# Reciprocal roots of the norms: ten VectorE steps replaced by one GpSimd power, and some diagonals made on ScalarE

## The chip, the core and the metric

The kernel runs on one core of one Trainium2 chip. The engines are named as the profile names them: PE (TensorE matmul; PEld is its weight load), DVE (VectorE), ACT (ScalarE), POOL (GpSimd) and SP (SyncE, which here issues nearly all DMAs). Each engine works through its own queue in order, and the queues wait for each other through semaphores. The metric is the device time of one execution in microseconds.

## What is computed

Two transformer layers on 512 rows of 1024 channels, with 256 rows of context beside them in the first layer. Layer 0 mixes with a gated chunk MLP and a differential attention of four heads; layer 1 with a windowed attention of 16 heads. Each layer ends in a SwiGLU of 2816 hidden channels. What matters here is the norm in front of nearly everything:

```python
def rmsnorm(x, g):
    xf = x.astype(jnp.float32)
    y = xf * lax.rsqrt(jnp.mean(xf * xf, axis=-1, keepdims=True) + EPS)
    return (y * g.astype(jnp.float32)).astype(x.dtype)
```

It stands at the entry of each layer, before each FFN, on the output of each head of layer 0 (over 128 channels), and at the end. The chunk MLP has a variance norm of its own, `lax.rsqrt(mean((vf - mu)^2) + EPS)`.

## The kernel before, in words

The activations lie transposed: a tile holds 128 channels on the partitions and up to 512 (rows) or 256 (context) positions along the free axis. Products are made in three passes (`mm3`, L99 to L101): a value is split into a high part in a reduced format, cast on ACT (L75, L115, L901), and a low rest, subtracted on POOL or DVE (L78, L116, L904), and high x high, high x low and low x high are summed. So every weight tile passes ACT and then POOL (or DVE) before PE can use it.

**A norm** has five steps. ACT squares the tiles and DVE or POOL add them up (`squares`, `square`, L183 and L769, L185 and L773). `rstd_diag` (L138) multiplies each block of 128 positions of the sums by a matrix of ones on PE (L149, L153), which leaves the sum of squares of position p on partition p; one DVE instruction takes the needed column of each block, scales it and adds epsilon (L156, or L158 for the heads, whose epsilon is a tensor). Then `rsqrt_small` (L124) takes the reciprocal root of these few columns, one per block of 128 positions: 2, 3, 4 or 6 of them. It starts from the bit trick (L128) and makes three Newton rounds of three DVE instructions each (L130, L131, L132), every one reading the one before. A diagonal matrix is built from each column by multiplying the identity with it, on DVE (L165). `spread` (L171) multiplies ones by the diagonals on PE (L175), which puts the factors of all positions on all partitions; the modulation or scaling reads them from there (L191, L599, L831, L1257, L1259).

There are 14 such norms, in order of time: rows and context at the entry (4 and 2 columns); the four heads of layer 0 (6 each); two halves before the FFN of layer 0 (3 each); rows and context at the entry of layer 1 (4 and 2); two halves before the FFN of layer 1 (2 each); two halves at the end (2 each). The chunk MLP calls the same `rsqrt_small` once through `rstd_small` (L118) on 24 columns.

**The FFN** (L842 on) computes each hidden tile f with a fast scheme of seven products (numbered 1 to 7) on sums and differences of the weights' and the inputs' quarters. The sums of weights are DVE instructions (L925). The second half's norm comes first in its order, "r", followed by products 2 and 1 of the tiles 0 to 2, which need only the first half; product 5 is the first that needs the second half modulated. In layer 0 the sums for product 5 of the first three tiles are tied behind the last diagonal of the norm:

```python
with tc.issue_after(self.last_diag.ins) if both and f < 3 and n == 5 else ExitStack():
    nc.vector.tensor_tensor(t, x, y, how)
```

**What sets the order.** The program is written for a tile framework, opened with `schedule_with_timeline_sim=True`. At build it simulates the engines with its own costs, gives an engine the ready instruction that stands earliest in the program (blocks under `high_priority` count as earlier), and so fixes the order of every queue; `issue_after` adds an edge by hand. On the chip that order doesn't change any more. An instruction that waits holds all that its engine has behind it.

Of the kernel before, what the change touches and what calls it, by code (L numbers as in the profile page):

```python
# [6 lines left out]
F32 = mybir.dt.float32  # L7
F32R = mybir.dt.float32r
BF16 = mybir.dt.bfloat16
I32 = mybir.dt.int32  # L10
AF = mybir.ActivationFunctionType
ALU = mybir.AluOpType
AX = mybir.AxisListType.X

P = 128
# [7 lines left out]
EPS = 1e-6  # L23
# [3 lines left out]
class Builder:  # L27
# [94 lines left out]
        return self.rsqrt_small(v, n, tag, 3)  # L122

    def rsqrt_small(self, v, n, tag="sm", bufs=6):  # L124

        ve = self.nc.vector
        y, t = self.small(n, tag, bufs), self.small(n, tag, bufs)
        ve.tensor_scalar(y.bitcast(I32), v.bitcast(I32), -0.5, float(0x5F3759DF), ALU.mult, ALU.add)  # L128
        for _ in range(3):
            ve.tensor_tensor(t, y, y, ALU.mult)  # L130
            ve.scalar_tensor_tensor(t, t, -0.5, v, ALU.mult, ALU.mult)  # L131
            ve.scalar_tensor_tensor(y, t, 1.5, y, ALU.add, ALU.mult)  # L132
        return y

    def rstd_rows(self, acc, T, inv, bank=None, dg=None, more=(), out=None):
# [2 lines left out]
    def rstd_diag(self, accs, inv, bank=None, eps=None, at=None, more=()):  # L138

        nc = self.nc  # L140
        nb = sum(T for _, T in accs) // P
        ms = self.small(nb)
        o = 0
        for acc, T in accs:
            ps = (bank or self.bank)()
            n = T // P
            for j in range(n):
                c = slice(j * P, (j + 1) * P)
                nc.tensor.matmul(ps[:, c], acc[:, c], self.ones, start=j == 0, stop=not more, skip_group_check=True)  # L149
            for t in more:  # L150
                for j in range(n):
                    c = slice(j * P, (j + 1) * P)
                    nc.tensor.matmul(ps[:, c], t[:, c], self.ones, start=False, stop=t is more[-1], skip_group_check=True)  # L153
            col = ps[:, 0:T].rearrange("p (j f) -> p j f", f=P)[:, :, 0]
            if eps is None:
                nc.vector.tensor_scalar(ms[:, o:o + n], col, inv, EPS, ALU.mult, ALU.add)  # L156
            else:
                nc.vector.scalar_tensor_tensor(ms[:, o:o + n], col, inv, eps[:, o:o + n], ALU.mult, ALU.add)  # L158
            o += n
        r = self.rsqrt_small(ms, nb)  # L160
        dgs, o = [], 0
        for acc, T in accs:
            dg = at if at is not None else self.tmp()
            for j in range(T // P):
                self.last_diag = nc.vector.tensor_scalar(dg[:, j * P:(j + 1) * P], self.ident, r[:, o + j:o + j + 1], None,  # L165
                                                         ALU.mult)
            dgs.append(dg[:, :T])
            o += T // P
        return dgs
# [119 lines left out]
    def consts(self):  # L289
        nc, a, p0 = self.nc, self.a, self.p0  # L290
        self.acc = [p0.tile([P, 96], F32, name=f"acc{i}") for i in range(2)]
        self.mod = [p0.tile([P, 96], F32, name=f"mod{i}") for i in range(2)]
        self.ones = p0.tile([P, P], F32, name="ones")
        nc.gpsimd.memset(self.ones, 1.0)
        warm = p0.tile([P, 1], F32, name="warm")
        nc.scalar.activation(warm, self.ones[:, 0:1], AF.Silu)

# [544 lines left out]
    def ffn(self, l):  # L842
        tc, nc, a = self.tc, self.nc, self.a
        both = l == 0
# [53 lines left out]
        def slot(src, t=None):  # L898
            t = ring.tile([P, 2, 512], F32R, name=self.uid("w"), tag="w", bufs=(6, 10)[l]) if t is None else t
            with tc.issue_after(self.first_sq.ins) if self.nslot < 12 else ExitStack():  # L900
                nc.scalar.copy(t[:, 0, :], src)  # L901
            self.nslot += 1
            eng = nc.vector if l == 1 and self.nslot % 4 == 0 else nc.gpsimd
            eng.tensor_tensor(t[:, 1, :], src, t[:, 0, :].bitcast(F32), ALU.subtract)  # L904
            return t
# [9 lines left out]
        def weights(n, f):  # L915
            if f not in raws:
                raws[f] = self.raws.pop(f) if f < 2 else self.ffn_in(l, f, ring if f % 3 == 2 else self.Rf)
                sums[f] = self.sumsq()[:, :512] if f % 3 == 2 else self.tmp("t")
            r, t = raws[f], sums[f]
            a11, a12, a21, a22 = [r[:, i * 512:(i + 1) * 512] for i in range(4)]  # L920
            for v, x, y, how in ((5, a21, a22, ALU.add), (6, t, a11, ALU.subtract), (3, a12, t, ALU.subtract),
                                 (7, a11, a21, ALU.subtract)):
                if v == n:
                    with tc.issue_after(self.last_diag.ins) if both and f < 3 and n == 5 else ExitStack():
                        nc.vector.tensor_tensor(t, x, y, how)  # L925
            return slot({1: a11, 2: a12, 4: a22}.get(n) if n in (1, 2, 4) else sums[f])

# [6 lines left out]
        def product(n, f):  # L934

            w = weights(n, f)
            st = state.setdefault(f, {})
            if n == 2:
# [398 lines left out]
```

## Time and profile before

| | |
|---|---|
| median of 3 runs | 1700.15 us (1699.94 to 1702.44) |
| the profiled execution | 1697.54 us, of which its span is 1695.8 |
| mean granted TensorE clock | 0.972 |
| PE, DVE, ACT, POOL busy | 1558.7, 1145.4, 752.8, 806.8 us |
| DMA, mean | 96 GB/s, queue q1 27.6% of 16 engines |

The profile names instructions by engine, line of the kernel and tile, as in `DVE L165 q<-ident,sm`. A timeline row has start and duration in us, engine, line, operation, output and inputs, shapes and the count of merged instructions; in brackets stands how long the engine had been idle before and what ended it. A row of waits has who waited for whom, the total in us, how often, and the longest. A row of one line's instructions has the count, then the shortest, median and longest duration in ns, then the first and last start. A row of groups has count, busy us, mean ns of one, and the idle time before. A row of windows has the stretch and its length, then busy us and count of PE, PEld, DVE, ACT and POOL, the granted clock, the DMA share and GB/s.

### The profile page before, as it was taken

The numbers are of one execution on the slowest core, as the hardware profiler recorded it, in microseconds if no ns is written. First come the engines' busy times: TensorE is split into PE (matmuls) and PEld (weight loads), VectorE is DVE, ScalarE is ACT, GpSimd is POOL, SyncE is SP. The second block draws the span as 40 slices with busy tenths as digits, with TensorE's granted clock in tenths as the row PEclk, the third lists the DMA queues.
The fourth block names the chain that finished last, engine by engine and source line by source line (L and its number), as shares of the span: only waits on it lengthen the run. The fifth ranks groups of instructions, "written<-read, shape, count | busy, mean of one in ns | idle before, by whom it ended". The sixth has DMA issues, their size and how long they took to land.

```text
span 1695.8 us, 24602 instructions
## 1 busy us (share of the span) xinstructions
PE 1558.7 (92%) x9415; PEld 1379.5 (81%) x9415; DVE 1145.4 (68%) x2037; ACT 752.8 (44%) x1521; POOL 806.8 (48%) x586
## 2 busy tenths in 40 slices
PE   6999989798899999999999988999987898999996
PEld 4776878698798889888899977778866788888986
DVE  4613788856967677666765676777769865756566
ACT  3413676433533233333333345676655444444443
POOL 0562211232675566656665336512115665666673
PEclk9999989899899899999999999999998999999998
DMA  8753100241032343344341112101140322222311
GB/s 312 290 184 133 32 1 1 87 159 41 25 125 88 124 136 110 127 136 135 132 132 38 49 63 75 51 7 45 50 146 10 125 90 98 87 100 78 110 38 50
DMA packets 47958, 161.98 MB, mean 96 GB/s; under 512 B 5472, under 2 KB 9952, under 8 KB 40160
## 3 DMA queue, kind: packets, MB, share of 16 engines
q1 hardware_dynamic: 47696, 160.28, 27.6%
q8 instruction: 74, 1.21, 0.3%
q14 instruction: 44, 0.36, 0.1%
q10 hardware_dynamic: 144, 0.13, 0.0%
HBM read 158.29 MB, written 2.10 MB: 95 GB/s over the span
## 4 chain that ended last, share of the span: by engine, by line
PE 65%; DVE 18%; DMA 6%; ACT 4%; issue 3%; POOL 3%; POOLq 0%; SPq 0%; DVEq 0%; ACTq 0%
PE pb L100 9%; PE pb L101 9%; PE pb L99 9%; PE pw L99 8%; PE pw L100 8%; PE pw L101 7%; DMA raw<-ffn_in 6%; POOL w L904 3%; DVE t L925 2%; PE pf L99 2%; PE pf L100 2%; PE pf L101 2%; PE pf L349 2%; DVE sq L925 1%; PE pb L1186 1%
## 5 line engine op out<-in xcount | busy, mean ns | idle before, releaser
L78 POOL TENSOR_TENSOR w<-raw,w 128x512 fp32r<-128x512 f32 (+1 forms) x84 | 128.6, 1540 | 234.3 <-ACT w L75 211.8
L99 PE MATMUL pw<-ax,w 128*128 128x384 f32 (+2 forms) x648 | 211.9, 331 | 18.0 <-DVE q L972 5.7
L904 POOL TENSOR_TENSOR w<-t,w 128x512 fp32r<-128x512 f32 x106 | 156.4, 1476 | 149.1 <-ACT w L901 146.0
L100 PE MATMUL pw<-ax,w 128*128 128x384 f32 (+2 forms) x648 | 210.7, 326 | 2.7 <-DVE ax L456 1.4
L101 PE MATMUL pw<-ax,w 128*128 128x384 f32 (+2 forms) x648 | 208.4, 324 | 3.1 <-DVE w L904 3.1
L757 DVE SCALAR_TENSOR_TENSOR xT<-pb,mod,xT 128x512 f32<-128x512 f32 (+3 forms) x208 | 143.9, 703 | 68.3 <-PE pb L101 67.9
L904 POOL TENSOR_TENSOR w<-raw,w 128x512 fp32r<-128x512 f32 x111 | 155.7, 1414 | 59.2 <-ACT w L901 59.2
L99 PE MATMUL pb<-hh,w 128*128 128x512 f32 x480 | 167.4, 363 | 14.8 <-ACT hh L115 7.9
L100 PE MATMUL pb<-hh,w 128*128 128x512 f32 x480 | 172.3, 361 | 0.7 <-POOL hh L116 0.2
L99 PE MATMUL pw<-T,w 128*128 128x384 f32 (+1 forms) x504 | 158.7, 318 | 12.2 <-DVE hs L968 9.5
L101 PE MATMUL pb<-hh,w 128*128 128x512 f32 x480 | 168.7, 359 | 0.0
L901 ACT CAST w<-t 128x512 fp32r<-128x512 f32 x120 | 74.2, 620 | 208.1 <-DVE t L925 176.8
L100 PE MATMUL pw<-T,w 128*128 128x384 f32 (+1 forms) x504 | 159.1, 316 | 7.0 <-DVE T L116 4.1
L101 PE MATMUL pw<-T,w 128*128 128x384 f32 (+1 forms) x504 | 158.3, 314 | 0.0
L99 PEld LDWEIGHTS pw<-ax,w 128*128 128x128 f32 x648 | 125.0, 194 | 32.8 <-DVE q L972 9.2
L100 PEld LDWEIGHTS pw<-ax,w 128*128 128x128 f32 x648 | 125.3, 193 | 10.5 <-DVE ax L193 3.3
L101 PEld LDWEIGHTS pw<-ax,w 128*128 128x128 f32 x648 | 124.8, 193 | 6.4 <-DVE w L904 3.3
L904 POOL TENSOR_TENSOR w<-rawo,w 128x512 fp32r<-128x512 f32 x74 | 107.2, 1448 | 39.1 <-ACT w L901 39.1
L99 PEld LDWEIGHTS pb<-hh,w 128*128 128x128 f32 x480 | 90.6, 191 | 28.5 <-ACT hh L115 9.0
L99 PEld LDWEIGHTS pw<-T,w 128*128 128x128 f32 x504 | 97.3, 194 | 18.9 <-DVE hs L968 11.9
L99 PE MATMUL pb<-ax,w 128*128 128x256 f32 (+1 forms) x344 | 106.8, 313 | 4.1 <-ACT w L75 2.2
L100 PE MATMUL pb<-ax,w 128*128 128x256 f32 (+1 forms) x344 | 106.3, 309 | 2.1 <-DVE ax L116 2.1
(381 smaller groups left out, 4324.4 us busy)
## 6 DMA issues: line engine op xcount, KB each, us to landing
raw<-ffn_in SPq DMA_DIRECT2D x44, 1024.0 KB, 5.7
ar<-ada SPq DMA_DIRECT2D x24, 1024.0 KB, 7.0
ar<-ada SPq DMA_DIRECT2D x48, 512.0 KB, 3.5
rawo<-ffn_out SPq DMA_DIRECT2D x44, 512.0 KB, 3.8
raw<-odd_out SPq DMA_DIRECT2D x32, 256.0 KB, 2.7
raw<-qk SPq DMA_DIRECT2D x16, 256.0 KB, 7.8
raw<-uv SPq DMA_DIRECT2D x16, 256.0 KB, 2.7
raw<-even_out SPq DMA_DIRECT2D x8, 512.0 KB, 3.5
```

The source lines that it names most:

```text
L78: eng.tensor_tensor(lo, raw, hi.bitcast(F32), ALU.subtract)
L99: mm(out, s[0], m[0], start=start, stop=False, **kw)
L100: mm(out, s[0], m[1], start=False, stop=False, **kw)
L101: mm(out, s[1], m[0], start=False, stop=stop, **kw)
L349: nc.tensor.matmul(ps[32 * q:32 * q + 32, :w], cst[:, k, :], t[:, w * q:w * q + w], start=k == 0, stop=k == KT - 1, skip_group_check=True)
L757: self.nc.vector.scalar_tensor_tensor(h, ps[:, r], self.modcol(l, j, m, who), h, ALU.mult, ALU.add)
L901: nc.scalar.copy(t[:, 0, :], src)
L904: eng.tensor_tensor(t[:, 1, :], src, t[:, 0, :].bitcast(F32), ALU.subtract)
L925: nc.vector.tensor_tensor(t, x, y, how)
L1186: nc.tensor.transpose(pt[:, x * P:(x + 1) * P], es[2 * (x % 2) + x // 2][:, kb * P:(kb + 1) * P], self.ident)
```

## The change

`rsqrt_small` becomes one POOL instruction: the columns to the power of a tile that holds -0.5 everywhere, set once at the start. The ten DVE instructions and the scratch tile go. The diagonals of the ten norms that have no epsilon tensor (26 blocks) are made on ACT, as a multiplication of the identity by a scalar per partition; those of the four heads (24 blocks) stay on DVE. The anchor for the three sums of weights in layer 0 moves from the last diagonal to the DVE instruction that writes the mean square.

```diff
     def rsqrt_small(self, v, n, tag="sm", bufs=6):
-
-        ve = self.nc.vector
-        y, t = self.small(n, tag, bufs), self.small(n, tag, bufs)
-        ve.tensor_scalar(y.bitcast(I32), v.bitcast(I32), -0.5, float(0x5F3759DF), ALU.mult, ALU.add)
-        for _ in range(3):
-            ve.tensor_tensor(t, y, y, ALU.mult)
-            ve.scalar_tensor_tensor(t, t, -0.5, v, ALU.mult, ALU.mult)
-            ve.scalar_tensor_tensor(y, t, 1.5, y, ALU.add, ALU.mult)
+        y = self.small(n, tag, bufs)
+        self.nc.gpsimd.tensor_tensor(y, v, self.mhalf[:, :v.shape[-1]], ALU.pow)
         return y
...
             if eps is None:
-                nc.vector.tensor_scalar(ms[:, o:o + n], col, inv, EPS, ALU.mult, ALU.add)
+                self.last_ms = nc.vector.tensor_scalar(ms[:, o:o + n], col, inv, EPS, ALU.mult, ALU.add)
...
             for j in range(T // P):
-                self.last_diag = nc.vector.tensor_scalar(dg[:, j * P:(j + 1) * P], self.ident, r[:, o + j:o + j + 1], None,
-                                                         ALU.mult)
+                c = slice(j * P, (j + 1) * P)
+                if eps is None:
+                    nc.scalar.mul(dg[:, c], self.ident, r[:, o + j:o + j + 1])
+                else:
+                    nc.vector.tensor_scalar(dg[:, c], self.ident, r[:, o + j:o + j + 1], None, ALU.mult)
...
         nc.gpsimd.memset(self.ones, 1.0)
+        self.mhalf = p0.tile([P, 24], F32, name="mhalf")
+        nc.gpsimd.memset(self.mhalf, -0.5)
...
-                    with tc.issue_after(self.last_diag.ins) if both and f < 3 and n == 5 else ExitStack():
+                    with tc.issue_after(self.last_ms.ins) if both and f < 3 and n == 5 else ExitStack():
```

## The prediction

> **What bounds the kernel now.** I read the page first (busy shares, clock, chain), then the waits of PE, then the timeline around each norm.
>
> ```profile
> span 1695.8 us, 24602 instructions
> ...
> PE 1558.7 (92%) x9415; PEld 1379.5 (81%) x9415; DVE 1145.4 (68%) x2037; ACT 752.8 (44%) x1521; POOL 806.8 (48%) x586
> ...
> PE 65%; DVE 18%; DMA 6%; ACT 4%; issue 3%; POOL 3%; POOLq 0%; SPq 0%; DVEq 0%; ACTq 0%
> ```
>
> PE is busy 92% of the span and owns 65% of the chain that ended last. So a change on DVE, POOL and ACT is worth only what PE waits for it. DVE owns 18% of that chain, and the norms are part of this share. The waits of PE name them:
>
> ```profile
> PE pf L649 <- DVE f L650: 7.4, 2, 6.9
> PE pb L175 <- DVE q L165: 6.3, 2, 3.7
> ...
> PE pw L101 <- DVE w L904: 3.1, 1, 3.1
> ```
>
> L165 is the diagonal at the end of a norm. L650 and L904 have nothing to do with a norm; they stand in DVE's queue behind one. The rows of two steps of the norm say why:
>
> ```profile
> L131 DVE SCALAR_TENSOR_TENSOR sm<-sm,sm x42: 144/161/2264, 15.1 to 1686.3; 128x2 f32<-128x2 f32 x18, 128x6 f32<-128x6 f32 x12, 128x4 f32<-128x4 f32 x6, 128x3 f32<-128x3 f32 x6
> L165 DVE TENSOR_SCALAR q<-ident,sm x46: 273/281/1827, 16.7 to 1290.3; 128x128 f32<-128x128 f32 x46
> ```
>
> A step on 2 to 6 columns takes 0.16 us at the median and 2.26 at worst, fourteen times as long on the same few columns. Ten such steps make a root, about 2 us when DVE has nothing else (some 0.2 from start to start).
>
> **The change, part by part.** There are 15 roots: 14 norms and the 24 columns of the chunk MLP. Each loses ten DVE steps, 150 in all. Each gains one POOL instruction on the same columns, with a hop from DVE to POOL and one onward. 26 of the 50 diagonals go from DVE to ACT; the 24 of the layer-0 heads stay. The three early weight sums of layer 0 (L925) are anchored behind the mean square instead of the diagonal. No DMA is added or moved, and the one memset of the exponents runs on POOL before its first work at 38.8 us, for nothing. The trace has no power, so its price P is bounded by POOL's other rows; next to them stands an ACT operation on 128x128:
>
> ```profile
> L78 POOL TENSOR_TENSOR w<-raw,w 128x1024 fp32r<-128x1024 f32 x8 | 21.0, 2655 | 8.6 <-ACT w L75 8.6
> ...
> L773 POOL TENSOR_TENSOR sq<-sq,sqs 128x256 f32<-128x256 f32 x9 | 6.6, 737 | 21.0 <-ACT sqs L769 20.6
> ...
> L769 ACT ACTIVATE q<-xT 128x128 f32<-128x128 f32 x5 | 1.5, 307 | 2.4 <-DVE xT L757 1.3 <-DVE sq L773 1.1
> ```
>
> From 256 to 1024 columns POOL adds 1.92 us, 2.5 ns a column, which leaves 0.1 us for none. As a plain product P would be about 0.11 us on 6 columns; the longest kind of row, 2.66 us, is the other end. I take 0.5 us, near the small end, since the columns are few and only the arithmetic per column is new. An ACT diagonal costs 0.31 us against DVE's 0.28: no gain and no loss by itself.
>
> Now the places, in order of weight.
>
> *Head 3 and the chunk MLP.*
>
> ```profile
> 329.45 2.26 DVE L131 SCALAR_TENSOR_TENSOR sm<-sm,sm 128x6 f32<-128x6 f32 x1
> ...
> 333.94 0.68 DVE L650 TENSOR_TENSOR f<-pf,sgub 128x512 f32<-128x512 f32 x1
> ```
>
> ```profile
> 325.25 4.14 POOL L116 TENSOR_TENSOR ax<-o,ax 128x768 fp32r<-128x768 f32 x2 [52.93 <-ACT ax L115]
> 329.35 4.64 POOL L78 TENSOR_TENSOR w<-raw,w 128x1024 fp32r<-128x1024 f32 x2
> ```
>
> ```profile
> 326.60 1.16 PE L649 MATMUL pf<-sguT,f 128*128 128x128 f32 x8 [0.46 <-ACT f L575]
> 334.67 1.22 PE L649 MATMUL pf<-sguT,f 128*128 128x128 f32 x4 [6.91 <-DVE f L650]
> 336.40 2.08 PE L649 MATMUL pf<-sguT,f 128*128 128x128 f32 x8 [0.52 <-DVE f L650]
> 339.56 1.77 PE L175 MATMUL pb<-q,ones 128*128 128x512 f32 x4
> ```
>
> ```profile
> 326.00:340.00 14.00, 6.11 (x27) 5.38 (x26) 13.12 (x21) 5.69 (x7) 7.99 (x4) 0.64 0.24 75
> ```
>
> The L131 step lasts 2.26 us, and a POOL instruction beside it 4.64/2 = 2.32: one DVE step gets in per POOL instruction. So the chain holds L650, which has its matmuls at 326.60 + 1.16 = 327.8, until 333.9. Without the chain L650 ends near 328.5 and PE goes on 6.1 us earlier. That cover then falls on L175: the power runs before L116 (325.1), behind it (329.4) or behind L78 (334.0); with P and six diagonals (1.7 us if not stretched) L175 could start at 327.3, 331.6 or 336.2 against 339.56. What is late next is this norm, if POOL's order puts it last. The last row gives the stretch from 326 to 340: PE busy 6.11 us of 14 and a mean granted clock of 0.64, so a shorter pause also spares slow matmuls; I count none of it. I take 4.5 us, ends 3 and 7.
>
> [...]
>
> *Second FFN norm, layer 0.*
>
> ```profile
> 415.13 0.16 DVE L156 TENSOR_SCALAR sm<-pb 128x3 f32<-128x3 f32 x1 [1.25 <-PE pb L153]
> ...
> 417.50 1.22 DVE L131 SCALAR_TENSOR_TENSOR sm<-sm,sm 128x3 f32<-128x3 f32 x1
> ```
>
> ```profile
> 414.92 7.49 POOL L904 TENSOR_TENSOR w<-raw,w 128x512 fp32r<-128x512 f32 x6 [0.84 <-ACT w L901]
> ```
>
> ```profile
> 424.07 0.88 PE L175 MATMUL pb<-q,ones 128*128 128x384 f32 x2 [3.70 <-DVE q L165]
> ```
>
> Again one step per L904 (7.49/6 = 1.25 us). Behind the first L904 the power ends at 414.92 + 1.25 + 0.5 = 416.7, three ACT diagonals (0.9) at 417.6 if ACT's casts let them; PE is free at 420.4 (424.07 - 3.70). The 3.7 us go, and DVE's three L925 sums run where the chain stood. Behind all six L904s it is 422.4 + 0.5 + 0.9 = 423.8: then only 0.3 us of PE's wait goes, though DVE is some 2 us ahead with the sums. ACT's diagonals wait for POOL, and casts behind them on ACT wait too. I take 4, ends 0.3 and 5.
>
> *Second FFN norm, layer 1.*
>
> ```profile
> 1284.54 0.68 DVE L904 TENSOR_TENSOR w<-raw,w 128x512 fp32r<-128x512 f32 x1
> ```
>
> ```profile
> 1279.08 7.27 POOL L904 TENSOR_TENSOR w<-raw,w 128x512 fp32r<-128x512 f32 x5 [21.86 <-ACT w L901]
> ```
>
> ```profile
> 1285.27 0.38 PE L101 MATMUL pw<-ax,w 128*128 128x256 f32 x1 [3.09 <-DVE w L904]
> ...
> 1295.25 0.50 PE L99 MATMUL pw<-T,w 128*128 128x256 f32 x2 [1.00 <-ACT T L115]
> ```
>
> DVE's own weight (L904) stands behind stretched steps. The 3.09 us go, and most of the 1.00 us, since the rescaled input comes earlier. 4, ends 3 and 5.
>
> *Entry of layer 1 and heads 0 to 2.*
>
> ```profile
> 980.65 1.89 DVE L165 TENSOR_SCALAR q<-ident,sm 128x128 f32<-128x128 f32 x4
> ```
>
> ```profile
> 982.68 1.10 PE L175 MATMUL pf<-q,ones 128*128 128x512 f32 x2 [1.41 <-DVE sm L156]
> ```
>
> ```profile
> 239.35 2.81 DVE L165 TENSOR_SCALAR q<-ident,sm 128x128 f32<-128x128 f32 x6
> ```
>
> ```profile
> 241.92 2.04 PE L175 MATMUL pb<-q,ones 128*128 128x512 f32 x2 [2.64 <-DVE q L165]
> ```
>
> At the entry 1.41 us go, and some 0.6 with the second norm's steps between DVE's modulations: 2, ends 1 and 3. In head 1 the 2.64 us in front of L175 go; the other heads' steps only thin DVE's queue. I take 3, ends 0 and 6 (attention is a tight exchange between PE, DVE and ACT).
>
> *The tail.*
>
> ```profile
> 1681.87 0.16 DVE L156 TENSOR_SCALAR sm<-pw 128x2 f32<-128x2 f32 x1 [0.27 <-PE pw L153]
> ```
>
> ```profile
> 1682.83 4.13 POOL L1257 TENSOR_TENSOR xT<-xT,rs 128x256 f32<-128x256 f32 x6 [3.29 <-ACT rs L1247]
> 1689.46 2.09 POOL L1257 TENSOR_TENSOR xT<-xT,rs 128x256 f32<-128x256 f32 x3 [2.49 <-ACT rs L1247]
> ```
>
> ```profile
> 1687.75 1.22 PE L175 MATMUL pf<-dg,ones 128*128 128x256 f32 x2 [5.40 <-DVE dg L165]
> ```
>
> The power fits between 1682.0 and POOL's start at 1682.83, and L175 starts near 1683.2 instead of 1687.75. Then POOL is late next: six and three products, 6.2 us and P. It loses its idle 2.49 at best: 2, ends 0 (power behind the six) and 4 (first half earlier as well).
>
> *Nothing* from the first norm, where DVE's root ends before PE's turn, nor from the context norm, the 24 columns and the first FFN norms, which have PE work in front of their L175 or L649. The covers are PE's work; in the first norm it is short:
>
> ```profile
> 14.48 0.16 DVE L156 TENSOR_SCALAR sm<-pb 128x4 f32<-128x4 f32 x1 [2.23 <-PE pb L149]
> ```
>
> ```profile
> 19.81 1.02 PE L175 MATMUL pb<-q,ones 128*128 128x512 f32 x2
> ```
>
> From 14.64, P and four ACT diagonals (1.2 us) have until 19.81: a P beyond 4.0 us costs there.
>
> *Against it:* two powers inside L904 streams push PE's weights by 0.5 us each, 1 us; and the order of every engine is planned anew at build, estimated at 0.5 us lost, between 4 gained and 4 lost.
>
> **Sum.** 4.5 + 4 + 4 + 2 + 3 + 2 = 19.5, less 1.5, is 18 us. The profiled execution took 1697.54 us (its span 1695.8 and 1.7 around it): 1679.5. The median of the runs shown, 1700.15, lies 2.6 above that execution, which would give 1682.1. I forecast 1681, between the two. The terms' ends with the new plan's give 7.3 - 1 - 4 = 2 to 30 - 1 + 4 = 33 us, 1666 to 1698.
>
> **Rivals.**
> *The power is queued late* on POOL at head 3, both second FFN norms and the tail. For it: POOL is full there (4.14 + 4.64, 7.49 and 7.27 us without a gap) and its order is fixed at build. Against: a norm stands earlier in the program than the weights beside it. L650 and L904 on DVE are freed all the same: 3 + 0.3 + 3 + 1 + 2 + 0 - 1.5 = 8 us, 1690.
>
> *A slow power* (slower than before). If P is several us, as an element-by-element routine would give, the first norm loses P - 4.0, the layer-0 FFN's weights are late by P and only the 3.70 us of waiting are there to pay with, P - 3.7, and layer 1 likewise P - 3.1. Head 3, heads 0 to 2 and the entry keep up to 9.5. It breaks even at 3P - 10.8 = 9.5, P = 6.8 us. At 10 us it loses 19.2, and 4.9 in the tail (1682.0 + 10 + 0.6 against 1687.75), less 9.5: 14.6 us slower, near 1714. For it: no row shows a power. Against: no POOL row on under 1024 columns is over 2.7 us.
>
> *A one-time wait before the first power.* Beyond 4.0 us it shows in the first norm, us for us; two us beyond give 1683. POOL's first product of the trace shows none that I can see. [...]
>
> *The new plan eats the gain*: PE's order changes in the stretches that were full, and nothing is left: 1700.
>
> **How the numbers follow.** Forecast as worked out (1670 to 1688) 0.53; late power (1688 to 1696) 0.17; one-time wait, inside the forecast's band, 0.04; new plan eats it (within 0.2%, 3.4 us of 1700.15, about what a measurement of this kernel can tell from no change) 0.07; slow power or a worse plan, over 1703.5, 0.16; a PE clock that no longer falls in the avoided waits, under 1670, 0.03. Faster 0.77, same 0.07, slower 0.16. The range 1669 to 1703 leaves out 0.16 above and some 0.03 below.
>
> **What would show it.** Right: one POOL instruction of about 0.5 us per norm, no DVE steps on sm; PE's wait for L650 below 2 us; no wait of L175 near 424; no wait for the DVE weight near 1285; L175 of the tail within 2 us of its L156. Wrong: P of over 2 us; POOL's weights waited for by PE where it did not; ACT idle before a diagonal with casts behind it.

## The result: 0.17% slower, and where the gain went

| | before | changed |
|---|---|---|
| median of 20 runs each | 1699.84 us | 1703.16 us |
| range | 1695.01 to 1705.5 | 1696.69 to 1709.37 |
| ratio, 95% interval | | 1.0017 (1.0007 to 1.0028) |
| the profiled execution | 1697.54 us | 1699.66 us |

The forecast was 1681. The kernel before was timed anew beside each batch of runs, and its median lies between 1697.14 and 1700.49 us; so kernels of different batches are compared below by their ratios, a thousandth of which is 1.7 us. The page of the changed kernel shows that DVE got what was meant for it, 39 us less work (1145.4 before), and that the time didn't follow: in the chain that ended last PE gave up 6 points, and POOL and "issue" took 3 each.

```profile
span 1697.9 us, 24501 instructions
...
PE 1552.8 (91%) x9415; PEld 1376.7 (81%) x9415; DVE 1106.5 (65%) x1861; ACT 761.2 (45%) x1547; POOL 824.5 (49%) x602
...
PE 59%; DVE 17%; DMA 6%; POOL 6%; issue 6%; ACT 5%; SPq 0%; POOLq 0%; DVEq 0%; ACTq 0%
```

**The price of a power**, from the groups of POOL by shape (busy us, then mean ns):

```profile
L126 POOL TENSOR_TENSOR sm<-sm,mhalf 128x6 f32<-128x6 f32 x4 | 5.4, 1350 | 31.1 <-DVE sm L152 30.4 <-PE pf L648 0.6
...
L126 POOL TENSOR_TENSOR sm<-sm,mhalf 128x2 f32<-128x2 f32 x6 | 5.1, 851 | 5.4 <-DVE sm L150 5.4
...
L126 POOL TENSOR_TENSOR sf<-sf,mhalf 128x24 f32<-128x24 f32 x1 | 4.2, 4163 | 13.8 <-DVE sf L121 13.8
```

0.85 us for 2 columns, 1.35 for 6, 4.16 for 24: some 0.15 us a column from 2 to 24 on a base of about 0.55. I had taken 0.5 for all.

**The waits of PE** in the changed kernel (us in all, times, longest). The wait for L649 (7.4 as L650 before) is down to 2.6 and the one for DVE's weight is gone, as forecast. New are the waits for POOL's hidden tiles, at most 3.9 at once (0.2 in all before), and one for a diagonal of head 3. The wait for a diagonal of the tail, 5.4 on DVE before, is 4.6 on ACT:

```profile
PE pb L100 <- POOL hh L116: 7.8, 8, 3.9
...
PE pf L172 <- ACT dg L161: 4.6, 1, 4.6
PE pb L172 <- DVE q L163: 4.6, 1, 4.6
...
PE pf L648 <- DVE f L649: 2.6, 1, 2.6
```

**Where the time went.** Each PE instruction of a kernel was paired with the same one (line and occurrence) in the profile of before; the median of the shift in its start over 25 us tells how far the kernel is ahead there; "at 400" means the 25 us that begin there. The table has how that shift changes from stage to stage, in us of one profiled execution each (minus is gained), by the clock of before. The changed kernel does gain at the norms, and loses more than ten us in 1325 to 1650, the bulk of the FFN of layer 1, where there is no norm and nothing was edited. The other rows are the experiments.

| kernel | head 3, chunk MLP (275-375) | 2nd norm, FFN 0 (375-475) | entry of layer 1 (925-1075) | 2nd norm, FFN 1 (1225-1325) | FFN 1 (1325-1650) | all the rest | span |
|---|---|---|---|---|---|---|---|
| **changed** | +2.1 | -1.6 | -5.8 | -2.5 | **+10.1** | -0.2 | +2.1 |
| e1 | +2.1 | -1.7 | -3.9 | -2.6 | -3.3 | -4.8 | -14.2 |
| e2 | -0.5 | -1.0 | -5.3 | -3.0 | -2.1 | -4.0 | -15.9 |
| e3 | +0.7 | -1.0 | -2.7 | -2.5 | **+16.5** | +0.9 | +11.9 |
| e4 | -7.4 | -1.7 | -6.0 | -4.0 | +0.8 | -0.1 | -18.4 |
| e5 | +2.1 | -1.7 | -2.9 | -3.9 | -1.6 | +0.5 | -7.5 |
| e6 | +0.1 | +1.9 | +1.5 | -1.0 | +0.5 | +1.0 | +4.0 |
| e7 | 0.0 | +5.8 | -2.2 | -0.5 | -0.4 | -2.0 | +0.7 |
| e8 | 0.0 | -0.9 | -5.8 | -2.4 | -2.2 | +3.3 | -8.0 |
| e9 | -0.8 | +3.1 | -0.1 | -0.2 | +0.3 | -0.7 | +1.6 |
| e10 | -7.4 | -1.7 | -5.9 | -3.7 | -3.0 | -5.8 | -27.5 |
| e11 | -4.8 | -1.7 | -4.8 | -3.5 | **+11.2** | 0.0 | -3.6 |
| e12 | -5.1 | -1.8 | -5.3 | -3.7 | -0.3 | -0.3 | -16.5 |

How much of a cell is chance is seen in e6, which is the kernel before up to 1290: up to 1.9. "All the rest" moves most in 475 to 925 (+0.6 to -3.9), with the same order in every kernel, so by chance too; over such a length it reaches some 4 us. The cells of "FFN 1" fall in two groups: +10.1 to +16.5, and -3.3 to +0.8.

**FFN 1 in the two profiles.** The waits of PE from 1330 to 1665, changed kernel first, then before; then one place of POOL's and PE's timeline, and POOL's of before:

```profile
PE pw L99 <- DVE hs L976: 7.7, 5, 2.6
PE pb L100 <- POOL hh L116: 6.8, 3, 3.9
PE pw L99 <- DVE hs L967: 6.8, 3, 2.8
```

```profile
PE pw L99 <- DVE q L972: 5.1, 4, 2.4
PE pw L99 <- DVE hs L977: 4.1, 3, 1.9
PE pw L99 <- DVE hs L968: 3.2, 2, 2.6
```

```profile
1644.09 3.40 POOL L903 TENSOR_TENSOR raw<-rawo,raw 128x512 fp32r<-128x512 f32 x2
1647.45 2.95 POOL L116 TENSOR_TENSOR hh<-hs,hh 128x512 fp32r<-128x512 f32 x2
```

```profile
1649.21 0.63 PE L100 MATMUL pb<-hh,w 128*128 128x512 f32 x1 [3.86 <-POOL hh L116]
1649.64 0.63 PE L101 MATMUL pb<-hh,w 128*128 128x512 f32 x1
...
1655.33 0.40 PE L100 MATMUL pb<-hh,w 128*128 128x512 f32 x1
```

```profile
1642.36 1.29 POOL L116 TENSOR_TENSOR hh<-hs,hh 128x512 fp32r<-128x512 f32 x1
```

In the changed kernel the split of a hidden tile (L116) stands behind two weights of 1.7 us in POOL's queue, and PE stands 3.86 us for it; before it ran between weights, and the waits of that stretch have no row for it. After the pause the matmuls take 0.63 us each instead of 0.40, and the granted clock is 0.64 from 1650 to 1654 us, 1.00 in the 4 us behind. Across this one place the shift goes from -2.3 to +3.3, so it costs 5.6 us. The other two kernels with a loss in this column have the same wait, 3.87 us, and lose 5.6 (e3) and 5.4 us (e11) there. All rows of that view add up to 26.3 us against 19.4, and PE's busy time (first number behind the length, with its count) is 152 ns an instruction against 150:

```profile
1330.00:1665.00 335.00, 308.54 (x2030) 281.76 (x2029) 202.67 (x286) 139.19 (x282) 202.28 (x149) 0.98 0.23 81
```

```profile
1330.00:1665.00 335.00, 315.53 (x2105) 287.04 (x2104) 214.77 (x302) 141.25 (x288) 207.12 (x151) 0.99 0.24 83
```

The two built programs differ there: from about 1360 to 1660 us PE, ACT, DVE and POOL of the changed kernel work in another order. Call before's order A and the changed kernel's B.

### The profile page after: what moved, and what is told of

The parts are those of the page before. It is cut to its first block, busy times and chain, and to the rows that moved or that the text cites. A ratio compares the mean times of both kernels' runs of the same rounds, so it can differ in the third digit from the quotient of the medians.

```text
span 1697.9 us, 24501 instructions
## 1 busy us (share of the span) xinstructions
PE 1552.8 (91%) x9415; PEld 1376.7 (81%) x9415; DVE 1106.5 (65%) x1861; ACT 761.2 (45%) x1547; POOL 824.5 (49%) x602
## 3 DMA queue, kind: packets, MB, share of 16 engines
q1 hardware_dynamic: 47696, 160.28, 27.5%
## 4 chain that ended last, share of the span: by engine, by line
PE 59%; DVE 17%; DMA 6%; POOL 6%; issue 6%; ACT 5%; SPq 0%; POOLq 0%; DVEq 0%; ACTq 0%
PE pb L100 8%; PE pb L99 8%; PE pb L101 8%; PE pw L99 7%; PE pw L101 7%; PE pw L100 7%; DMA raw<-ffn_in 5%; POOL w L903 5%; PE pf L99 2%; PE pf L100 2%; PE pf L101 2%; DVE t L924 2%; PE pf L348 2%; PE pb L1185 1%; DVE junk L217 1%
## 5 line engine op out<-in xcount | busy, mean ns | idle before, releaser
L903 POOL TENSOR_TENSOR w<-t,w 128x512 fp32r<-128x512 f32 x106 | 156.1, 1473 | 141.8 <-ACT w L900 136.4
L78 POOL TENSOR_TENSOR w<-raw,w 128x512 fp32r<-128x512 f32 (+1 forms) x84 | 125.2, 1499 | 202.5 <-ACT w L75 178.6
L903 POOL TENSOR_TENSOR w<-raw,w 128x512 fp32r<-128x512 f32 x111 | 155.2, 1409 | 61.4 <-ACT w L900 60.1
L99 PE MATMUL pb<-hh,w 128*128 128x512 f32 x480 | 166.9, 362 | 16.5 <-ACT hh L115 6.9
L903 POOL TENSOR_TENSOR w<-rawo,w 128x512 fp32r<-128x512 f32 x74 | 108.9, 1472 | 34.0 <-ACT w L900 34.0
```

The lines of the kernel that those rows point to most:

```text
L78: eng.tensor_tensor(lo, raw, hi.bitcast(F32), ALU.subtract)
L99: mm(out, s[0], m[0], start=start, stop=False, **kw)
```

## Theory, rivals and the experiments

*Theory "order"*: the gains at the norms are real; B, which the build came to as a side effect, loses them. *Rival "given back"*: the FFN is paced by DVE, ACT and POOL, and any lead of PE is waited for again. *Rival "power"*: the powers and their hops are what costs.

For the experiments each norm got a name, and two lists say what it uses; with all names in POWER and the ten norms without an epsilon tensor in DACT this is the changed kernel. Old Newton steps and DVE diagonals stand where a name is missing.

```diff
+NORMS = ["first", "ctx", "ffn0a", "ffn0b", "entry1a", "entry1b", "ffn1a", "ffn1b", "tail_a", "tail_b"]
     def rsqrt_small(self, v, n, tag="sm", bufs=6, kind=None):
+        if kind not in POWER:
...
         y = self.small(n, tag, bufs)
         self.nc.gpsimd.tensor_tensor(y, v, self.mhalf[:, :v.shape[-1]], ALU.pow)
...
-                if eps is None:
+                if kind in DACT:
                     nc.scalar.mul(dg[:, c], self.ident, r[:, o + j:o + j + 1])
```

**e1, one covered norm put back.**

```diff
-POWER = [... "ffn1a", "ffn1b" ...]; DACT = [... "ffn1a", "ffn1b" ...]
+POWER = [... "ffn1b" ...]; DACT = [... "ffn1b" ...]
```

> The changed kernel with one norm put back: the first half before the FFN of layer 1 has its Newton steps and DVE diagonals again, 13 of 14 norms and the 24 columns keep the power. That norm has PE work in front of it and cost nothing in either kernel; but with it put back, the static order of PE, ACT and POOL from about 1360 to 1660 us is again that of the kernel before, while the changed kernel has another one there. Theory 'order': the changed kernel is some 7 us ahead of the one before at 1330 us and loses this, and more, by 1650 in an order that is worse; with the old order it keeps 4 to 8 us: 1692 to 1697, 0.995 to 0.998 of the time before. Rival 'given back': the FFN is paced by DVE, ACT and POOL, and what PE has gained is waited for again whatever the order; then this is the changed kernel's time, 1.001 to 1.003. Rival 'power': the powers themselves and their hops cost what is lost; they are all but one still there, so also 1.001 to 1.003.

Measured: 1686.64 us, 0.9937 (0.9914 to 0.9961), a little better than expected. By the ratios that is 13.6 us less than the changed kernel, from undoing a norm for which PE had not waited. The FFN of layer 1 goes from +10.1 to -3.3. Neither rival can account for that; whether it is the norm that was put back or the order that came with it is asked in e5.

**e2, three places only.**

```diff
+POWER = DACT = ["ffn0b", "entry1a", "entry1b", "ffn1b"]
```

> The kernel before, with power and ACT diagonals only at three places: the second halves before both FFNs and the entry of layer 1, and the anchor of the changed kernel. The static order of the long FFN stretches stays that of before (PE differs from it only around those three places). Theory 'order': the gains seen there in the changed kernel (about 4, 5 and 8 us, with 2 to 3 of the first and up to 6 of the last given back within 25 us where DVE's modulation paces) remain to the end: 6 to 10 us, 1690 to 1694, 0.994 to 0.997. Rival 'given back': 0.999 to 1.001.

Measured: 1685.13 us, 0.9925 (0.9904 to 0.9946), more than expected. These four of 14 norms give all that e1 gets from 13 and the 24 columns.

**e3, the 24 columns as Newton steps.**

```diff
-POWER = [... "head", "sf" ...]
+POWER = [... "head" ...]
```

> The changed kernel with the root of the 24 columns of the chunk MLP as Newton steps on DVE again; the static order of the FFN of layer 1 stays that of the changed kernel. The power on 24 columns took 4.16 us there, the ten DVE steps 2.2 us before, and DVE then had 24 normalizations in a row to do for which PE waited. Theory 'the 24-column power is on the path': the stretch from 320 to 345 us gets 1.5 to 2 us shorter, and the whole 1701, 1.0005 of the time before. Rival 'hidden': no change, 1703, 1.0017.

Measured: 1703.71 us, 1.0035 (1.002 to 1.0051). Head 3's stretch gets 1.4 us shorter (e1 and e5, the same there as the changed kernel, have its +2.1 again), so the 24-column power was on the path. The whole, above both expectations, shows nothing of it, and the order is still B. B's stretch varies by more than that between executions, +10.1 and +16.5 in these two. The place in the changed kernel, POOL, then DVE:

```profile
319.73 4.16 POOL L126 TENSOR_TENSOR sf<-sf,mhalf 128x24 f32<-128x24 f32 x1 [13.84 <-DVE sf L121]
...
330.77 1.36 POOL L126 TENSOR_TENSOR sm<-sm,mhalf 128x6 f32<-128x6 f32 x1 [0.56 <-PE pf L648]
```

```profile
305.92 1.27 DVE L163 TENSOR_SCALAR q<-ident,sm 128x128 f32<-128x128 f32 x6
...
323.93 6.37 DVE L647 TENSOR_SCALAR f<-f,mv,sf 128x128 f32<-128x128 f32 x18 [4.28 <-POOL sf L126]
...
332.75 0.69 DVE L649 TENSOR_TENSOR f<-pf,sgub 128x512 f32<-128x512 f32 x1
333.36 6.45 DVE L163 TENSOR_SCALAR q<-ident,sm 128x128 f32<-128x128 f32 x6
339.73 0.41 DVE L649 TENSOR_TENSOR f<-pf,sgub 128x256 f32<-128x256 f32 x1
```

The first L649 no longer waits behind Newton steps, but the second now stands behind the six diagonals that stayed on DVE: 6.45 us beside POOL's L116 and L78, where the six of head 2, at 305.92, took 1.27.

**e4, the heads' diagonals on ACT too.**

```diff
-POWER = [... "head", "sf" ...]; DACT = NORMS
+POWER = [... "head" ...]; DACT = NORMS + ["head"]
```

> The changed kernel with the 24-column root as Newton steps again, and the diagonals of the four heads on ACT too. In the changed kernel the six diagonals of head 3 stayed on DVE and took 6.45 us, one per POOL instruction, in front of the second L649 for which PE waited. Theory 'the choke moved from the steps to the diagonals': between 318 and 345 us another 3 to 5 us go beside the 2 of the 24 columns. The static order of the FFN of layer 1 is that of the kernel before again in this build, so by 'order' all adds up: 1700 - 5 - 6 = 1689, range 1686 to 1693, 0.992 to 0.996. Rival 'given back': within 1.000 to 1.002. Rival for the heads: ACT, which in attention makes the exponentials, is late by the diagonals, and the stretch 220 to 345 is no shorter than in the changed kernel.

Measured: 1678.31 us, 0.9881 (0.9858 to 0.9905), more than expected. Head 3's stretch gains 7.4 us, 8.1 more than e3's. Now DVE has both L649 (here L664) early, and ACT makes the diagonals in 1.86 us while POOL's L119 (L116 before) runs, from 330.62 to 332.44:

```profile
329.62 0.69 DVE L664 TENSOR_TENSOR f<-pf,sgub 128x512 f32<-128x512 f32 x1 [1.97 <-PE pf L663]
331.12 0.42 DVE L664 TENSOR_TENSOR f<-pf,sgub 128x256 f32<-128x256 f32 x1 [0.80 <-PE pf L663]
```

```profile
330.67 1.86 ACT L176 ACTIVATE q<-ident,sm 128x128 f32<-128x128 f32 x6 [1.42 <-POOL sm L138]
```

**e5, the changed kernel and one matmul more.**

```diff
+        self.nsp = getattr(self, 'nsp', 0) + 1
+        for _ in range(2 if self.nsp == 16 else 1):
             self.nc.tensor.matmul(out[:, :T], self.ones, dg, start=True, stop=True)
```

> The changed kernel with nothing put back and one instruction more: the matmul that spreads the factors of the second half before the FFN of layer 1 is issued twice, the second writing the same values again (0.4 us of PE). With this the build gives PE, ACT, DVE and POOL the order of the kernel before again from about 1380 to 1660 us; up to 1280 us the orders are those of the changed kernel. Theory 'order': though it does more, it is 10 us or more faster than the changed kernel: 1685 to 1690, 0.992 to 0.996 of the time before. Rival 'it was the first half's power or its diagonals' (put back in the first experiment, here still there): no gain, 1.001 to 1.004.

Measured: 1687.45 us, 0.9933 (0.9913 to 0.9953). Nothing is undone, one instruction is added, and by the ratios 14.3 us go: the FFN of layer 1 is at -1.6, and POOL's hidden tile costs 0.2 us in that stretch. This is the strongest evidence for the theory: the same work in order A.

```profile
PE pb L100 <- POOL hh L116: 0.2, 1, 0.2
```

**e6, the kernel before with the same matmul four times.** The edit is that of e5, on before, with 4 for 2.

> The kernel before, no power and no ACT diagonal, with the same spread matmul issued four times instead of once (1.2 us of PE more). The build gives another order than either kernel's between about 1290 and 1440 us, and that of before elsewhere. Theory 'order': without any change of the norms the time moves by more than the 1.2 us, by 2 to 8 us, of either sign (0.994 to 1.005, outside 0.9995 to 1.0015). Rival 'orders are worth little as such, only that of the changed kernel's last tiles is bad': +1 us, 1.0005.

Measured: 1701.02 us, 1.0005 (0.999 to 1.002). The rival holds: this third order, in 1290 to 1440 us, can't be told from none, within -1.7 to +3.4 us. Not every new order costs; B does.

**e7, only the diagonals of the three places.**

```diff
+POWER = []
+DACT = ["ffn0b", "entry1a", "entry1b", "ffn1b"]
```

> The kernel before with only the diagonals of the three places (second halves before both FFNs, entry of layer 1) on ACT; all roots stay Newton steps on DVE. PE's order differs from before only around the second half of layer 0 and the entry of layer 1. Theory 'the power is what frees DVE': the ten steps still go one per POOL instruction, so 0 to 2 us at most: 0.999 to 1.000. Rival 'the diagonals were the choke, as at head 3': a good part of the 12 us of the three places with power, 4 us or more: under 0.998.

Measured: 1701.19 us, 1.002 (1.0004 to 1.0035): no gain, rather a loss, in the order A. The gain of the three places needs the power. The loss stands at the second norm of layer 0 (+5.8), where this kernel has the changed anchor, which lets DVE's sums in between the Newton steps; so at that place a gain by the diagonals alone can't be told from the anchor's loss. The -2.2 at the entry of layer 1 is hardly more than chance (e6: +1.5).

**e8, power at the three places, Newton steps and ACT diagonals at the heads.**

```diff
+POWER = ["ffn0b", "entry1a", "entry1b", "ffn1b"]
+DACT = ["ffn0b", "entry1a", "entry1b", "ffn1b", "head"]
```

> The three places with power and ACT diagonals as in the second experiment, and at the heads Newton steps on DVE with the diagonals on ACT; all other norms as before. At head 3 this asks whether the power was needed beside the ACT diagonals. Theory 'both are needed, each alone leaves a choke on DVE': the ten steps stand in front of L649 as before (6 us), so head 3 gives 0 to 1.5 us and the whole is that of the three places, 0.992 to 0.9935. Rival 'the diagonals alone were it': 7 us as with power and ACT diagonals, 0.988 to 0.990.

Measured: 1687.92 us, 0.993 (0.9909 to 0.9951), the time of the three places: head 3 gains nothing. The Newton steps hold the first L649 again, and PE waits 6.99 us, as before:

```profile
333.39 2.26 DVE L134 SCALAR_TENSOR_TENSOR sm<-sm,sm 128x6 f32<-128x6 f32 x1
335.68 2.26 DVE L135 SCALAR_TENSOR_TENSOR sm<-sm,sm 128x6 f32<-128x6 f32 x1
337.87 0.68 DVE L664 TENSOR_TENSOR f<-pf,sgub 128x512 f32<-128x512 f32 x1
```

```profile
338.60 1.22 PE L663 MATMUL pf<-sguT,f 128*128 128x128 f32 x4 [6.99 <-DVE f L664]
```

With e3 (power, DVE diagonals: +0.7), e8 (Newton, ACT diagonals: 0.0) and e4 (both: -7.4) the square is full but for its first corner, which is before: either edit alone is worth nothing there.

**e9, each power twice**, on the kernel of e4.

```diff
+        for _ in range(2):
             self.nc.gpsimd.tensor_tensor(y, v, self.mhalf[:, :v.shape[-1]], ALU.pow)
```

> The kernel of the fourth experiment (24 columns as Newton steps, all diagonals on ACT, order of before in the FFN of layer 1) with each of the 14 powers issued twice, the second writing the same columns again: P goes from 0.85 to 1.4 us to twice that. The long stretches of the FFN of layer 1 keep the order of before. Theory 'P is cheap where it stands': only the places where PE waits for the norm pay, some five of them (three heads, head 3, tail) by about 1 us each: 3 to 6 us, 1681 to 1684 on the scale of that kernel's 1678, ratio 0.990 to 0.992. Rival 'each power is on the path': 14 times about 1.1 us, 15 us, ratio 0.996 to 0.998. Rival 'all hidden': no change, 0.988.

Measured: 1695.85 us, 0.9973 (0.996 to 0.9986), by the ratios 15.6 us over e4: the size of the second expectation, but not by its mechanism. The covered norms lose nothing; the four places in the table lose 6.6, 4.8, 5.9 and 3.8 us, far more than one more P. The second power isn't always next to the first. In POOL's queue at the second norm of layer 0 three weights stand between:

```profile
415.83 1.30 POOL L139 TENSOR_TENSOR sm<-sm,mhalf 128x3 f32<-128x3 f32 x1
417.11 4.19 POOL L919 TENSOR_TENSOR w<-raw,w 128x512 fp32r<-128x512 f32 x3
421.26 0.85 POOL L139 TENSOR_TENSOR sm<-sm,mhalf 128x3 f32<-128x3 f32 x1
```

So this shows about what the rival of a late power would have cost, and doesn't price P by itself. PE's order is another one at these places too, so not all of the loss need be the late power.

**e10, power where PE had waited.**

```diff
+POWER = DACT = ["ffn0b", "entry1a", "entry1b", "ffn1b", "head", "tail_a", "tail_b"]
```

> Power and ACT diagonals only where PE waited: the four heads, the second halves before both FFNs, the entry of layer 1 and the end; the first norm, the context norm, the first halves before the FFNs and the 24 columns stay Newton steps and DVE diagonals. Order of before in the FFN of layer 1. Theory 'the covered norms give nothing either way': the time of the fourth experiment within 2 us, 0.987 to 0.9895. Rival 'the powers at covered norms cost at the start' (the changed kernel is 1.5 us late from 40 us on): 1 to 2 us faster than the fourth experiment, 0.986 to 0.988.

Measured: 1672.99 us, 0.9847 (0.9822 to 0.9871), the fastest of all and faster than either expectation. Its interval overlaps that of e4; that it is better is likely and not shown, and most of what it has on e4 in the profile lies where their orders agree, 475 to 925 and 1325 to 1650 us.

**e11 and e12, the kernel of e10 with the context norm's spread issued two and three times.** The edit is that of e5 at the second spread, with 2 and with 3.

> The kernel of the tenth experiment (power at the useful places) with one instruction more: the spread matmul of the context norm at about 45 us is issued twice (0.6 us of PE). The build then gives the FFN of layer 1 the order that it has in the changed kernel. Theory 'order': the stretch from 1325 to 1650 us gets some 10 to 16 us longer than in the tenth, and the whole 1683 to 1690, 0.990 to 0.994. Rival 'that order is only bad together with the first half's power or what else the changed kernel has': 0.984 to 0.986, as the tenth.

> As the eleventh, but the matmul is issued three times. With still one more instruction the order in the FFN of layer 1 is that of the kernel before again (but for 4 rows of PE's). Theory 'order': back to the time of the tenth within 3 us, 0.983 to 0.987, though more work is done than in the eleventh. Rival: slower than the eleventh or the same, since it does more.

Measured: e11 1697.7 us, 0.9987 (0.9972 to 1.0003); e12 1678.93 us, 0.9873 (0.9856 to 0.9891). One matmul at 45 us brings B, and by the ratios it costs 23.8 us against e10; a second one takes 19.4 of them back. In e11 the FFN of layer 1 is at +11.2, 14.2 above e10's and within the 10 to 16 expected, with POOL's hidden tile back among PE's waits of that stretch; in e12 it is at -0.3. The whole of e11 is slower than the 0.990 to 0.994 expected, so B isn't all of its loss: in the profiles 5.8 us of the difference to e10 lie ahead of 375 us, where the matmul changes the order as well, and 2.5 us in 475 to 925 us, where it doesn't. e12 is 4.4 us above e10 by the ratios, where at most 3 were expected; the intervals overlap.

```profile
PE pb L103 <- POOL hh L119: 4.4, 2, 3.9
```

## Why the prediction was wrong, step by step

**The step that failed** is the last term: the order of every engine is planned anew, "estimated at 0.5 us lost, between 4 gained and 4 lost". The new order of the FFN of layer 1 cost +10.1 us in the profiled execution; by the ratios the changed kernel is 14.3 us slower than the same work in order A (e5). Its bounds came from no row. As a rival it stood with 1700 and a chance of 0.07; it is what happened, and it wasn't in the stretches beside the norms but in one without any. With order A the changed kernel is at 0.9933, 11 us faster than before, against 18 forecast. Most of the other 7 lies in two terms that failed as well:

*Head 3, 4.5 us forecast, none came.* The root did leave L650's way. But I priced the six diagonals at "1.7 us if not stretched" and the 24 columns at nothing, though my own row of L165 had a longest diagonal of 1.83 us for a median of 0.28. The diagonals took 6.45 us on DVE (six took 1.27 at head 2), in front of the second L649, and the 24-column power 4.16, of which 1.4 showed (e3). Of the +2.1 in the table, 1.5 arise by 300 us, ahead of head 3. I had asked which norm is late next and not what else of it stays on the choked engine. Of the six diagonals the first three took 1.26, 2.38 and 2.38 us, from 333.4 us on, while POOL's L116 and two L78 ran until 339.1; the other three took 0.27 to 0.28 us each, and the six of head 2, with POOL idle, 0.28 to 0.29. What held the three up isn't shown.

*Heads 0 to 2, 3 us forecast, none came.* From 175 to 275 us, where head 0's norm stands, the shift changes by +0.2 in the changed kernel, and by -1.2, +0.1 and 0.0 in e1, e3 and e5 with the same heads; with ACT diagonals and Newton steps (e8) it is +2.6. The 2.64 us in front of L175 at 241.92, which are head 0's and not head 1's, did go: the diagonals started at 232.79 instead of 239.35. But PE then waited for ACT's exponentials, from 225 to 262 us 5.9 us instead of 0.7; over the whole kernel, before and changed:

```profile
PE pw L532 <- ACT e L536: 4.7, 4, 1.7
```

```profile
PE pw L531 <- ACT e L535: 8.9, 5, 3.6
```

This is the tight exchange that the prediction had as the reason for an end of 0. Heads 1 and 2 had no wait in front of their L175. Another 1.5 us are lost from 275 to 300 us (1.4 to 1.5 in e1, e3 and e5), where PE waits 1.40 us at 298.61 for a DVE instruction of L116; no run separates what made that one late.

**What was right.** *Second FFN norm, layer 0*: the power stands behind one L903, L172 doesn't wait:

```profile
418.86 1.30 POOL L903 TENSOR_TENSOR w<-raw,w 128x512 fp32r<-128x512 f32 x1 [0.89 <-POOL ax L116]
420.12 1.30 POOL L126 TENSOR_TENSOR sm<-sm,mhalf 128x3 f32<-128x3 f32 x1
421.39 6.75 POOL L903 TENSOR_TENSOR w<-raw,w 128x512 fp32r<-128x512 f32 x5
```

```profile
424.98 0.81 PE L172 MATMUL pb<-q,ones 128*128 128x384 f32 x2
```

From +3.9 at 400 the shift falls to -0.4 at 425, the forecast 4; by 475 it is +2.2 again, where PE waits 4.24 us for DVE's hidden sums (L967) instead of 2.55, so 1 to 2 stay. *Second FFN norm, layer 1*: the same, a lead of 11.9 us at 1300 that is 6.8 at 1325; of the forecast 4, 2.4 to 4.0 stay. *Entry of layer 1*: 2 forecast, 2.7 to 6.0 measured with the power, the one term that was too small. From 975 to 1012 us PE's waits for the modulated rows (1.6 and 1.3 us) went beside the 1.41, and 2.2 us for an ACT diagonal are new; what made the rest isn't shown. *Tail*: forecast 2, found 1.2, with the second power behind the six products, the term's own lower case:

```profile
1684.52 4.14 POOL L1256 TENSOR_TENSOR xT<-xT,rs 128x256 f32<-128x256 f32 x6 [1.49 <-ACT rs L1246]
...
1688.62 0.70 POOL L126 TENSOR_TENSOR sm<-sm,mhalf 128x2 f32<-128x2 f32 x1
```

```profile
1690.11 0.98 PE L172 MATMUL pf<-dg,ones 128*128 128x256 f32 x2 [4.58 <-ACT dg L161]
```

*P*: 0.85 to 1.35 for 0.5, of no weight where it was queued early. The slow power and a one-time wait at it did not come: the first power, at 14.29 us, took 1.02 us, as the other on 4 columns. It began 0.16 us behind the end of the DVE instruction that writes its columns (L150, 13.97 + 0.16). The two instructions that configure POOL stand at 1.2 us in the trace, 13 us ahead of it; a wait in that gap could have passed unseen.

**Open:** why the build falls into A or B. Repeated matmuls of 0.4 to 1.2 us, at 45 us or just ahead of that stretch, tip it either way. And what makes the rest of B's loss: 5.6 of the 10.1 us are the one late hidden tile, its wait and the slow matmuls behind it, as are 5.6 of 16.5 in e3 and 5.4 of 11.2 in e11; the remaining 4.5, 10.9 and 5.8 us are spread over 1325 to 1643 us and aren't accounted for.

## What to carry to other kernels

Where a build plans the order, an edit can cost more in a stretch that it doesn't touch than it gains where it acts: compare the orders of the two programs stage by stage, and try the edit with a harmless nudge (an instruction issued twice) before judging it. Take work off a choked engine completely or not at all: at head 3 the root without the diagonals gave nothing (+0.7, e3), and so did the diagonals without the root (0.0, e8); both gave 7.4 us (e4). Put it first where the critical engine waits for it: four such norms (e2) gave as much as 13 norms and the 24 columns (e1).

## What was not expected of the hardware

A power on GpSimd cost some 0.15 us per column on 128 partitions (0.85 us for 2, 4.16 for 24), 60 times the 2.5 ns per column between its plain sums and differences of 256 and 1024 columns (0.74 and 2.66 us). On DVE the multiplication of one 128x128 tile by a column took 1.26 to 2.38 us beside POOL's work at head 3 for 0.28 with POOL idle, as in the kernel before a Newton step took 2.26 there for 0.16; on ACT, beside POOL's L119, six took 1.86 us, 0.31 for each (e4), and four with POOL idle 1.28 (changed kernel, at 15.34). The pause of PE at 1645 cost more than its length: behind the 3.86 us the matmuls took 0.63 us for 0.40, at a granted clock of 0.64, and 5.6 us were lost in all.
